# One layer of a hybrid decoder on one core: a fourth raw weight buffer, later second tables, a sum moved to VectorE and another order at the end

## The chip, the cores and the metric

The kernel runs on one core of one Trainium2 chip, in one launch. The metric is the device time of an execution in microseconds (us), told as the median of three runs. A profiled execution has its own time and a span: the span goes from the first recorded instruction to the last, and its own time is the span and the little that lies around it.

## What is computed

One decoder layer for 256 tokens of width 1024, in float32:

```python
h = x
h = h + hybrid_mixer(rmsnorm(h), ...)      # two attention branches, gates, output projection
h = h + peer_ffn(rmsnorm(h), wq, subkeys, u, v)
return rmsnorm(h, norm_final)

# peer_ffn: 128*128 = 16384 experts, 8 heads, 16 experts kept per head and token
q   = hf @ wq                              # scores against 2 x 128 subkeys per head
idx, w = top16 of the sums of two top16, softmax
act = gelu(einsum('cd,chkd->chk', x_c, u[idx]))
out = einsum('chk,chkd->cd', w * act, v[idx])
```

`u` and `v` have 16384 rows of 1024 numbers each, 64 MB apiece. The mixer takes some 270 us of the kernel; the change lies in the expert part.

## The kernel before, in words

**Weights.** All weight matrices are cut to blocks of 128 x 1024 float32 (512 KB) that stand in one list, `order`; the last 256 of them are 128 blocks of u and 128 of v. For each block SyncE (SP) issues one DMA into a tile `raw` (`fetch`, L184); ScalarE (ACT) rounds it to `whi` (L195) and VectorE (DVE) subtracts, `wlo = raw - whi` (L199), so that TensorE (PE) can multiply in two parts that together hold full precision. The pool `stream` has three buffers each for `raw`, `whi` and `wlo`. A `raw` buffer is free when `wlo` is made; a `whi` buffer when PE is through with that block. `slot` (L238) is the unit of the hand-written order: slot k issues the loads of blocks k+2 and k+3, makes `whi` and `wlo` of block k+2, runs what else is planned for this slot (lists `first`, `pre`, `late`, `early`), and then emits PE's matmuls for block k. The engines run their own rows in order and are tied by semaphores alone.

**u side.** Two blocks make a pair (`u_pair`): each block is multiplied with all tokens but the first 32 (24 matmuls of 224 columns, L367), the pair's result goes through Gelu to `G` (L1225, or L1219 and L1221). In the first half (64 blocks) the routing runs beside it: `steps` is a list of (estimated us, function) for top-16 searches, softmax, index lookups (`look_...`, ending in `idx`, L1047) and gathered dots; `advance(PACE)` at each slot gives it credit. `tables(b)` (L1049) transposes the weights and both index lists of token block b on PE (L1052) and copies them out. In the second half one-hot products (`hot_...`, L1294, L1309) multiply the routing weights into `G`.

**The first 32 tokens** are done otherwise: 32 times a row of u per partition (128 rows of 4 KB) is gathered by GpSimd (POOL) with an indirect DMA (L1086), `dot` (L1096) multiplies it on DVE with the tokens and gives a sum per row, and later 32 gathers of v are summed into `ysum` (`row_sum`, L1380). Dots 0 to 12 lie in the first half of u with three buffers, dots 13 to 21 in the second half and 22 to 31 in the first slots of the v side with two buffers `row0`, `row1` (`rows_wide`). Each dot or row_sum issues the gather that takes its buffer next (`rows_next`). After the last row_sum a chain on POOL folds the four parts (`fold_in`, `fold` L1392, `few_in` L1401 to L1403), `few_add` (L1406, POOL) adds the residual, `few_square` (L1409, ACT) and `few_factor` (L1414, ACT) give the norm, `few_out` (L1418 to L1424) writes the 32 rows. They are put at fixed slots of the v side by `at_slot`.

**v side.** Per block 8 matmuls of 448 columns with `whi` (`v_high`, L1345) and 8 of 224 with `wlo` (`v_low`, L1349) go into 8 PSUM banks `acc`; the moving operand `co` is made from `G` by ACT (L1258) and DVE (L1259) two slots ahead. The last two blocks are multiplied bank by bank (`finish`), DVE adds the residual (L1460, L1462), PE turns the rows (`turn_rows`, L1466), ACT sums squares (`total`, L1476), and norm and output follow (L1482 to L1518).

Of the kernel before, what the change touches and what calls it, by code (L numbers as in the profile page):

```python
# [31 lines left out]
PACE = 1.26  # L32
# [6 lines left out]
FETCH = 18  # L39
TD = T - NG  # L40
# [100 lines left out]
def body(tc, nc, a):  # L141
# [6 lines left out]
    ps = PP.enter_context(tc.tile_pool(name="ps", bufs=2, space=PSUM))  # L148
    PA = ExitStack()
# [22 lines left out]
    raws, parts, at = {}, {}, [0]  # L172

    def fetch(k):
        if k in raws or k >= len(order):
            return
        ap = order[k]
        t = stream.tile([P, D], F32, name="raw")
        if len(ap.shape) == 3:
            t = t[:, :ap.shape[1] * ap.shape[2]]  # L180
        raws[k] = t
        o = t if len(ap.shape) == 2 else t.rearrange("p (a b) -> p a b", a=ap.shape[1])
        if k:
# [54 lines left out]
    def slot(use, first=(), pre=()):  # L238
        k = at[0]
        fetch(k + 2)  # L240
        fetch(k + 3)
# [77 lines left out]
    ah = const.tile([P, NC, T], F32R)  # L319
    al = const.tile([P, NC, T], F32R)  # L320
# [760 lines left out]
    def rows_of_step(n):  # L1081
        return rows_at[n % 3] if n < DOTS[0] else rows_wide[n % 2]
# [6 lines left out]
    def rows_next(n):  # L1089
        m = n + (3 if n < DOTS[0] else 2)  # L1090
        if m < (DOTS[0] if n < DOTS[0] else 2 * NG):
            rows_in(m)
# [31 lines left out]
    steps.append((0.5, tables, 1))  # L1124
    first_dot = next(k for k, v in enumerate(steps) if v[1:] == (soft_sub, 1))
    ahead, behind = steps[:first_dot], steps[first_dot:]
    share, done, n = sum(v[0] for v in behind) / DOTS[0], 0.0, 0
    for v in behind:
        ahead.append(v)
        done += v[0]  # L1130
        while n < DOTS[0] and done >= share * (n + 0.5):
            ahead.append((1.35, dot, n))
            n += 1
    steps = ahead
# [47 lines left out]
    for m in range(8):  # L1182
        first, second = [], []
        if m:
# [8 lines left out]
            if m > 1:  # L1193
                first.append(lambda: advance(1.3))
                second.append(lambda: advance(0.6 if m == 2 else 1.2))
# [55 lines left out]
    rows_wide += [wide_rows.tile([P, D], F32, name=f"row{k}") for k in range(2)]  # L1251
# [8 lines left out]

    OH = ExitStack()
# [65 lines left out]
    for k in range(2):  # L1327
        at_slot(3 + 2 * k, "pre", rows_in, DOTS[0] + k)
# [8 lines left out]
    OH.close()  # L1337
    oh = top.enter_context(tc.tile_pool(name="ov", bufs=2, reuse_waits="tile"))
# [3 lines left out]
    small = slice(TD, 2 * TD)  # L1342

# [61 lines left out]
    def few_add():  # L1405
        nc.gpsimd.tensor_tensor(few[0], few[0], few[1], OP.add)  # L1406
# [18 lines left out]

    for n in range(DOTS[1], NG):
# [43 lines left out]
    sq = [oh.tile([P, 2], F32, name="lsq")[:TB] for b in range(2)]  # L1470
# [4 lines left out]
    def total(b, d):  # L1475
        nc.scalar.activation(whole, turned[2 * d + b][:TB], AF.Square, scale=1.0 / 32.0, accum_out=sq[b][:, d:d + 1])  # L1476
# [15 lines left out]
    def guard(b):  # L1492
        nc.vector.tensor_scalar(sums[b][:, 0:1], sq[b][:, 0:1], EPS, None, OP.add)

    rows_of = lambda b: a["out"][NG + b * TB:NG + (b + 1) * TB]
    for c in range(NC):
# [38 lines left out]
```

## Time and profile before

| | us |
|---|---|
| median of three runs (996.63, 1001.39, 1002.73) | 1001.39 |
| profiled execution, its own time | 995.05 |
| its span | 993.3 |
| u side, second half, first to last matmul | 464 to 651.6 |
| v side, first matmul L1345 to the first of `finish` | 651.59 to 974.87 |
| last output DMA issued | 987.72 |

All times within the execution count from the start of the span. A row of the chain or of a timeline is start, duration, engine, line, operation, output<-inputs; in brackets stands how long the engine was idle before it and what ended that. A row of a waits list is total us, times, longest. In a row of stretches the busy time and number of instructions of each engine come first, then the clock that TensorE was granted (1.00 is full), the mean busy share of the 16 DMA engines, and GB/s. PE's matmuls are pipelined: a busy PE shows only that work was in it.

### The profile page before, as it was taken

How to read it: one execution, taken by the hardware profiler on the slowest of the kernel's cores; microseconds unless marked ns; L12 is line 12 of the kernel's file. 1: busy time of each engine (PE TensorE's matmuls, PEld its weight loads, DVE VectorE, ACT ScalarE, POOL GpSimd, SP SyncE). 2: the span in 40 equal slices, each digit the busy share in tenths (PEclk: the TensorE clock that was granted, in tenths of full speed). 3: DMA queues.
4: the chain of work that ended last, by engine and by line, in shares of the span. 5: the costliest groups of instructions: out<-in, count | busy, mean ns of one | idle time of the engine just before them, and what ended most of it. 6: DMA issues, size and time to landing. Idle time of an engine off the chain costs nothing.

```text
span 993.3 us, 20220 instructions
## 1 busy us (share of the span) xinstructions
PE 971.9 (98%) x7825; PEld 940.1 (95%) x7825; DVE 793.9 (80%) x1485; ACT 591.1 (60%) x1069; POOL 130.8 (13%) x114
## 2 busy tenths in 40 slices
PE   9999999999999999999999999999999999999995
PEld 7898999999999999999999999999899999999985
DVE  5788877877989989877889999777777787777756
ACT  7545544656554655647888888655455555555553
POOL 3000110000000021221001001012212222223210
PEclk9999999999999999999999999999999999999998
DMA  8733344566556668877556555667888888888762
GB/s 276 255 94 119 109 116 144 170 197 176 182 182 213 217 205 276 300 261 239 197 182 208 191 192 191 212 230 258 274 280 288 279 307 284 285 296 300 267 213 82
DMA packets 61425, 217.24 MB, mean 219 GB/s; under 512 B 7121, under 2 KB 8321, under 8 KB 61321
## 3 DMA queue, kind: packets, MB, share of 16 engines
q1 hardware_dynamic: 48352, 174.42, 54.3%
q0 software_dynamic: 11280, 39.68, 11.4%
q10 hardware_dynamic: 1696, 1.84, 0.6%
q8 instruction: 62, 1.02, 0.4%
q14 instruction: 35, 0.28, 0.1%
HBM read 212.86 MB, written 2.52 MB: 217 GB/s over the span
## 4 chain that ended last, share of the span: by engine, by line
PE 56%; DMA 21%; DVE 13%; issue 5%; ACT 4%; POOL 1%; ACTq 0%; DVEq 0%; POOLq 0%
PE pj L367 45%; DMA raw<-in_v_n 16%; DVE wlo L199 6%; ACT whi L195 4%; PE pw L1294 3%; DMA raw<-in_u_t 2%; DVE ysum L1380 1%; DVE co L1259 1%; PE pS L660 1%; DMA xq<-ys 1%; PE pS L499 1%; PE pT L632 1%; PE acc L1345 1%; DMA row<-xrd 1%; DVE row L1096 1%
## 5 line engine op out<-in xcount | busy, mean ns | idle before, releaser
L199 DVE TENSOR_TENSOR wlo<-raw,whi 128x1024 fp32r<-128x1024 f32 (+2 forms) x329 | 398.3, 1211 | 131.7 <-ACT whi L195 130.1
L195 ACT ACTIVATE whi<-raw 128x1024 fp32r<-128x1024 f32 (+2 forms) x329 | 345.7, 1051 | 247.7 <-DMA raw<-in_v_n 92.9
L367 PE MATMUL pj<-ah,whi 128*128 128x224 f32 (+1 forms) x1344 | 320.6, 282 | 1.3 <-ACT ah L326 0.7
L367 PE MATMUL pj<-al,whi 128*128 128x224 f32 (+1 forms) x1344 | 314.9, 277 | 0.4 <-DVE al L327 0.4
L367 PEld LDWEIGHTS pj<-ah,whi 128*128 128x128 f32 x1344 | 257.4, 191 | 3.2 <-ACT ah L326 1.2
L367 PEld LDWEIGHTS pj<-al,whi 128*128 128x128 f32 x1344 | 258.0, 192 | 2.0 <-issue 1.0
L1345 PE MATMUL acc<-co,whi 128*128 128x448 f32 x1024 | 232.7, 368 | 4.4 <-ACT whi L195 4.3
L1345 PEld LDWEIGHTS acc<-co,whi 128*128 128x128 f32 x1024 | 183.3, 189 | 17.5 <-ACT whi L195 5.7
L367 PE MATMUL pj<-ah,wlo 128*128 128x224 f32 (+1 forms) x1344 | 181.5, 277 | 0.0
L367 PEld LDWEIGHTS pj<-ah,wlo 128*128 128x128 f32 x1344 | 166.7, 192 | 0.0
L1349 PEld LDWEIGHTS acc<-co,wlo 128*128 128x128 f32 x1024 | 134.9, 191 | 4.2 <-DVE wlo L199 0.9
L1349 PE MATMUL acc<-co,wlo 128*128 128x224 f32 x1024 | 136.2, 273 | 0.6 <-DVE wlo L199 0.6
L1282 ACT ACTIVATE onehot<-onehot,wl 128x128 f16<-128x128 f16 x224 | 71.3, 393 | 6.1 <-DVE onehot L1286 3.9
L1086 POOL DMA_INDIRECT row<-in_v_n,sidx x32 | 51.6, 1612 | 157.8 <-DVE ysum L1380 116.8
L1258 ACT ACTIVATE co<-G 128x224 fp32r<-128x224 f32 x128 | 48.8, 382 | 32.1 <-PE acc L1349 31.4
L1086 POOL DMA_INDIRECT row<-in_u_n,sidx x19 | 29.7, 1565 | 225.1 <-DVE row L1096 224.5
L1259 DVE TENSOR_TENSOR co<-G,co 128x224 fp32r<-128x224 f32 x128 | 49.7, 389 | 8.9 <-ACT co L1258 8.9
L367 PE MATMUL pj<-bh,whi 128*128 128x256 f32 x192 | 48.0, 286 | 0.0
L367 PE MATMUL pj<-bl,whi 128*128 128x256 f32 x192 | 47.4, 284 | 0.0
L1380 DVE SCALAR_TENSOR_TENSOR ysum<-row,acts,ysum 128x1024 f32<-128x1024 f32 x31 | 39.6, 1279 | 0.0
L627 ACT ACTIVATE prob<-pS,nm 128x128 f32<-128x128 f32 (+1 forms) x48 | 19.8, 416 | 30.6 <-DVE nm L624 30.6
L367 PEld LDWEIGHTS pj<-bl,whi 128*128 128x128 f32 x192 | 36.5, 190 | 0.0
(323 smaller groups left out, 931.1 us busy)
## 6 DMA issues: line engine op xcount, KB each, us to landing
raw<-in_u_t SPq DMA_DIRECT2D x128, 512.0 KB, 3.6
raw<-in_v_n SPq DMA_DIRECT2D x128, 512.0 KB, 4.7
raw<-in_w_m SPq DMA_DIRECT2D x16, 512.0 KB, 3.6
raw<-in_w_q SPq DMA_DIRECT2D x16, 512.0 KB, 3.7
raw<-in_w_t SPq DMA_DIRECT2D x15, 512.0 KB, 4.6
raw<-in_w_b SPq DMA_DIRECT2D x8, 512.0 KB, 3.5
raw<-in_w_o SPq DMA_DIRECT2D x8, 512.0 KB, 3.5
sg<-in_w SPq DMA_DIRECT2D x4, 512.0 KB, 6.5
```

Source lines behind the costliest of these rows:

```text
L195: return [lambda s=slice(u, min(v, n)): nc.scalar.activation(hi[:, s], raws[k][:, s], AF.Copy) for u, v in cuts]
L199: nc.vector.tensor_tensor(lo[:, cs], raws[k][:, cs], hi[:, cs].bitcast(F32), OP.subtract)
L367: nc.tensor.matmul(out, (wl if v == 2 else wh)[:, c], (l if v == 1 else h)[:, c], start=(i == 0), stop=(i == len(seq) - 1))
L627: nc.scalar.activation(p[:, o], src[b], AF.Exp, bias=nm[:, b:b + 1], accum_out=sums[:, b, h:h + 1])
L1086: nc.gpsimd.indirect_dma_start(rows_of_step(n), None, src, bass.IndirectOffsetOnAxis(ap=sidx[:, n % NG:n % NG + 1], axis=0))
L1258: nc.scalar.activation(t[:, :TD], g, AF.Copy)
L1259: nc.vector.tensor_tensor(t[:, TD:], g, t[:, :TD].bitcast(F32), OP.subtract)
L1282: nc.scalar.activation(E[:, 1, t], E[:, 1, t], AF.Copy, scale=wl[:, n:n + 1])
L1294: nc.tensor.matmul(pw[:, t * P:(t + 1) * P], E[:, 0, t], E[:, 2 - s, t], start=(s == 0), stop=(s == 1))
L1345: nc.tensor.matmul(acc[c][:, :2 * TD], w[0][:, c * P:(c + 1) * P], coefs[k], start=(k == 0), stop=False, skip_group_check=True)
L1349: nc.tensor.matmul(acc[c][:, small], w[1][:, c * P:(c + 1) * P], coefs[k][:, :TD], start=False, stop=(k == P - 1), skip_group_check=True)
L1380: nc.vector.scalar_tensor_tensor(ysum, t, w, ysum, OP.mult, OP.add)
```

## The change

**Four raw buffers.** From block 67 of u on, of every four weight blocks three go to the pool `stream` as before and the fourth to a spare buffer in the pool `rows`; from the second half of u on, `slot` issues the loads of blocks k+2 to k+4. **One row buffer in the second half of u.** Only `row0` is there; the second, `row1`, is made at the start of the v side in the pool that takes the place of the one-hot tiles, and its first gather (row 23) is issued in slot 0 there. `ah` and `al` (the tokens in two parts) move to a pool of their own that closes after the u side. **Second tables last.** `tables(1)` stands at the end of `steps`, behind all dots; `PACE` is 1.29 for 1.26, and the last of the eight query pairs gives less credit. **The gathered tokens' sum** (`few_add`) is made by DVE, in slot 118 instead of 112; the table load for the square root, `few_square`, `few_factor` and `few_out` come five slots later each, `few_in` one. **The end.** In `finish` both `whi` products come ahead of both `wlo` products, the residual is added to the large part first, and the squares of the second half of the columns are summed in two pieces (384 and 128 columns).

```diff
-PACE = 1.26
+PACE = 1.29
+SPARE = 1
...
+    spares, V0, ahead = [], len(order) - P - 61, [3]
     def fetch(k):
...
-        t = stream.tile([P, D], F32, name="raw")
+        spare = spares and (k - V0) % (3 + SPARE) >= 3
+        t = (spares[0] if spare else stream).tile([P, D], F32, name="raw", **({"bufs": SPARE} if spare else {}))
...
     def slot(use, first=(), pre=()):
         k = at[0]
-        fetch(k + 2)
-        fetch(k + 3)
+        for n in range(2, ahead[0] + 1):
+            fetch(k + n)
...
     def rows_of_step(n):
-        return rows_at[n % 3] if n < DOTS[0] else rows_wide[n % 2]
+        return rows_at[n % 3] if n < DOTS[0] else rows_wide[n % len(rows_wide)]
...
     def rows_next(n):
-        m = n + (3 if n < DOTS[0] else 2)
+        m = n + (3 if n < DOTS[0] else len(rows_wide))
...
-    steps.append((0.5, tables, 1))
...
-    steps = ahead
+    steps = front + [(0.5, tables, 1)]
...
-                first.append(lambda: advance(1.3))
-                second.append(lambda: advance(0.6 if m == 2 else 1.2))
+                first.append(lambda: advance(1.3 if m < 7 else 1.0))
+                second.append(lambda: advance(0.6 if m in (2, 7) else 1.2))
...
-    rows_wide += [wide_rows.tile([P, D], F32, name=f"row{k}") for k in range(2)]
+    rows_wide.append(wide_rows.tile([P, D], F32, name="row0"))
...
+    spares.append(wide_rows)
+    ahead[0] = 3 + SPARE
...
-    for k in range(2):
-        at_slot(3 + 2 * k, "pre", rows_in, DOTS[0] + k)
+    at_slot(3, "pre", rows_in, DOTS[0])
...
     OH.close()
+    HX.close()
...
+    rows_wide.append(oh.tile([P, D], F32, name="row1", bufs=1))
...
     def few_add():
-        nc.gpsimd.tensor_tensor(few[0], few[0], few[1], OP.add)
+        nc.vector.tensor_tensor(few[0], few[0], few[1], OP.add)
...
+    at_slot(0, "v", rows_in, DOTS[1] + 1)
...
-    at_slot(n + 4, "v", few_in)
-    at_slot(n + 6, "v", few_add)
-    at_slot(n + 9, "v", lambda: table(AF.Sqrt))
-    at_slot(n + 10, "v", few_square)
-    at_slot(n + 11, "v", few_factor)
-    at_slot(n + 13, "v", few_out)
+    at_slot(n + 5, "v", few_in)
+    at_slot(n + 12, "v", few_add)
+    at_slot(n + 14, "v", lambda: table(AF.Sqrt))
+    at_slot(n + 15, "v", few_square)
+    at_slot(n + 16, "v", few_factor)
+    at_slot(n + 18, "v", few_out)
...
     def finish(c):
-        for k in (P - 2, P - 1):
-            v_high(k, ends[k], c)
-            v_low(k, ends[k], c)
+        for f in (v_high, v_low):
+            for k in (P - 2, P - 1):
+                f(k, ends[k], c)
         xc = x2c(c)[:, NG:]
-        nc.vector.tensor_tensor(xc, xc, acc[c][:, small], OP.add)
         lasts[c] = oh.tile([P, TD], F32, name="last", bufs=3)
-        nc.vector.tensor_tensor(lasts[c], acc[c][:, :TD], xc, OP.add)
+        nc.vector.tensor_tensor(xc, xc, acc[c][:, :TD], OP.add)
+        nc.vector.tensor_tensor(lasts[c], acc[c][:, small], xc, OP.add)
...
     turn_rows(6)
+    for b in range(2):
+        total(b, 4, 7, 1)
     turn_rows(7)
     for b in range(2):
+        gained(b, 0)
         guard(b)
-        gained(b, 0)
     for b in range(2):
-        total(b, 1)
+        total(b, 7, 8, 2)
         root(b)
```

How the change moves rows is shown at three places. The first is DVE at the end of the first half of u, where the last index list `idx` is made; `wlo` rows are the weight blocks, `xg` and `g_wide` rows are dots, `wl` belongs to `tables(1)`. Before:

```order
L199 TENSOR_TENSOR wlo<-raw,whi 128x1024 [waits DMAHW6_49,PE_49,Activation_49]
L1096 SCALAR_TENSOR_TENSOR g_wide,acts<-g_wide,xq 128x1024 [waits DMASW0_49]
L199 TENSOR_TENSOR wlo<-raw,whi 128x1024 [waits DMAHW7_49,PE_49,Activation_49]
L1046 TENSOR_TENSOR sc<-sc 128x8x32 [waits DVE_49]
L1047 TENSOR_TENSOR idx<-sc 128x128 [waits DVE_49]
L1061 SCALAR_TENSOR_TENSOR wl<-pO,wt 128x128 [waits PE_49,Activation_49]
L199 TENSOR_TENSOR wlo<-raw,whi 128x1024 [waits DMAHW0_49,Activation_49]
L1096 SCALAR_TENSOR_TENSOR xg,acts<-xg,xq 128x1024 [waits DMASW1_49]
```

And now:

```order
L204 TENSOR_TENSOR wlo<-raw,whi 128x1024 [waits DMAHW6_49,PE_49,Activation_49]
L1101 SCALAR_TENSOR_TENSOR g_wide,acts<-g_wide,xq 128x1024 [waits DMASW0_49]
L1051 TENSOR_TENSOR sc<-sc 128x8x32 [waits DVE_49]
L1052 TENSOR_TENSOR idx<-sc 128x128 [waits DVE_49]
L204 TENSOR_TENSOR wlo<-raw,whi 128x1024 [waits DMAHW7_49,PE_49,Activation_49]
L1101 SCALAR_TENSOR_TENSOR xg,acts<-xg,xq 128x1024 [waits DMASW1_49]
L204 TENSOR_TENSOR wlo<-raw,whi 128x1024 [waits DMAHW0_49,PE_49,Activation_49]
L1066 SCALAR_TENSOR_TENSOR wl<-pO,wt 128x128 [waits PE_49,Activation_49]
```

`idx` is one weight block earlier on DVE, and the last dot and the table's own row have changed places. On PE the three transposes of `tables(1)` stand one weight block (24 matmuls) later than before.

The second place is ACT near the end of the v side, slots 115 to 117 before: the table load, the square of the 32 rows and the root. Before:

```order
L195 ACTIVATE whi<-raw 128x1024 [waits DMAHW5_49,DVE_49]
L280 ACT_TABLE_LOAD
L280 ACTIVATE junk<-ones 128x1
L1258 ACTIVATE co<-G_5867 128x224 [waits DVE_49,PE_49]
L195 ACTIVATE whi<-raw 128x1024 [waits DMAHW6_49,DVE_49]
L1409 ACTIVATE row_5872,fs<-row_5871 32x1024 [waits DMASW4_49,DMASW5_49,DMASW2_49,Pool_49]
L1258 ACTIVATE co<-G_5867 128x224 [waits DVE_49,PE_49]
```

Now, at slots 120 to 122:

```order
L200 ACTIVATE whi<-raw 128x1024 [waits DMAHW2_49,DVE_49]
L285 ACT_TABLE_LOAD
L285 ACTIVATE junk<-ones 128x1
L1262 ACTIVATE co<-G_5870 128x224 [waits DVE_49,PE_49]
L200 ACTIVATE whi<-raw 128x1024 [waits DMAHW3_49,DVE_49]
L1416 ACTIVATE row_8860,fs<-row_5874 32x1024 [waits DMASW4_49,DMASW5_49,DMASW2_49,DVE_49]
L1262 ACTIVATE co<-G_5870 128x224 [waits DVE_49,PE_49]
```

The square waits for DVE, no longer for POOL, and stands five blocks later; the row that it waits for stands on DVE three blocks ahead of it.

The third place is PE at the start of `finish`, the last two blocks of v, first two banks (the numbers behind the names are buffers: `whi_12070` and `wlo_12071` are the last block but one, `whi_12093` and `wlo_12094` the last). Before:

```order
L1345 MATMUL acc_8855<-co_12067,whi_12070 128x448
L1349 MATMUL acc_8855<-co_12067,wlo_12071 128x224
L1345 MATMUL acc_8855<-co_12090,whi_12093 128x448
L1349 MATMUL acc_8855<-co_12090,wlo_12094 128x224
L1345 MATMUL acc_8854<-co_12067,whi_12070 128x448
L1349 MATMUL acc_8854<-co_12067,wlo_12071 128x224
```

Now (`whi_12067` and `wlo_12068` the last block but one, `whi_12097` and `wlo_12098` the last):

```order
L1352 MATMUL acc_8859<-co_12064,whi_12067 128x448
L1352 MATMUL acc_8859<-co_12094,whi_12097 128x448
L1356 MATMUL acc_8859<-co_12064,wlo_12068 128x224
L1356 MATMUL acc_8859<-co_12094,wlo_12098 128x224
L1352 MATMUL acc_8858<-co_12064,whi_12067 128x448
L1352 MATMUL acc_8858<-co_12094,whi_12097 128x448
```

The product with the last `whi` moves from the third place of a bank to the second; the one with the last `wlo` stays the fourth. SP's list of loads and POOL's list of gathers keep their order, but that rows 23 and later are asked for at other steps; POOL loses the sum.

More of the change, by code (lines that the diff above doesn't have):

```diff
@@ L148, in body @@
     ps = PP.enter_context(tc.tile_pool(name="ps", bufs=2, space=PSUM))
+    HX = ExitStack()
+    hx = HX.enter_context(tc.tile_pool(name="hx", bufs=1, side="right", reuse_waits="tile"))
     PA = ExitStack()
@@ L318, in body @@
     x2c = lambda c: x2[c // 4][:, c % 4]
-    ah = const.tile([P, NC, T], F32R)
-    al = const.tile([P, NC, T], F32R)
+    ah = hx.tile([P, NC, T], F32R, name="ah")
+    al = hx.tile([P, NC, T], F32R, name="al")
     bh = pa.tile([P, NC, T], F32R)
@@ L1123, in body @@
             steps.append((0.3, route))
-    steps.append((0.5, tables, 1))
     first_dot = next(k for k, v in enumerate(steps) if v[1:] == (soft_sub, 1))
-    ahead, behind = steps[:first_dot], steps[first_dot:]
+    front, behind = steps[:first_dot], steps[first_dot:]
     share, done, n = sum(v[0] for v in behind) / DOTS[0], 0.0, 0
     for v in behind:
-        ahead.append(v)
+        front.append(v)
         done += v[0]
         while n < DOTS[0] and done >= share * (n + 0.5):
-            ahead.append((1.35, dot, n))
+            front.append((1.35, dot, n))
             n += 1
-    steps = ahead
+    steps = front + [(0.5, tables, 1)]
     credit = [0.0]
@@ L1424, in few_out @@
         nc.gpsimd.dma_start(a["out"][0:NG], few[0])
+    assert DOTS[1] % 2 == 0
+    at_slot(0, "v", rows_in, DOTS[1] + 1)
     for n in range(DOTS[1], NG):
@@ L1469, in body @@
     yo = [stream.tile([P, D], F32, name="raw")[:TB] for b in range(2)]
-    sq = [oh.tile([P, 2], F32, name="lsq")[:TB] for b in range(2)]
+    sq = [oh.tile([P, 4], F32, name="lsq")[:TB] for b in range(2)]
     sums = [oh.tile([P, 4], F32, name="lr")[:TB] for b in range(2)]
@@ L1473, in body, with total @@
     whole = rows_wide[1][:TB, 0:512]
-    def total(b, d):
-        nc.scalar.activation(whole, turned[2 * d + b][:TB], AF.Square, scale=1.0 / 32.0, accum_out=sq[b][:, d:d + 1])
+    def total(b, c0, c1, n):
+        d = c0 // 4
+        cs = slice((c0 - 4 * d) * P, (c1 - 4 * d) * P)
+        nc.scalar.activation(whole[:, cs], turned[2 * d + b][:TB, cs], AF.Square, scale=1.0 / 32.0,
+                             accum_out=sq[b][:, n:n + 1])
     def gained(b, d):
@@ L1481, in root @@
     def root(b):
-        nc.scalar.activation(sums[b][:, 1:2], sq[b][:, 1:2], AF.Sqrt, bias=sums[b][:, 0:1])
+        nc.scalar.activation(sums[b][:, 1:2], sq[b][:, 2:3], AF.Sqrt, bias=sums[b][:, 0:1])
     def factor(b):
         e, r, w, t = (sums[b][:, k:k + 1] for k in range(4))
-        nc.vector.tensor_scalar(w, sq[b][:, 1:2], e, -0.5, OP.add, OP.mult)
+        nc.vector.tensor_scalar(w, sq[b][:, 2:3], e, -0.5, OP.add, OP.mult)
         nc.vector.reciprocal(r, r)
@@ L1492, in guard @@
     def guard(b):
-        nc.vector.tensor_scalar(sums[b][:, 0:1], sq[b][:, 0:1], EPS, None, OP.add)
+        nc.vector.scalar_tensor_tensor(sums[b][:, 0:1], sq[b][:, 0:1], EPS, sq[b][:, 1:2], OP.add, OP.add)
     rows_of = lambda b: a["out"][NG + b * TB:NG + (b + 1) * TB]
@@ L1501, in body @@
             for b in range(2):
-                total(b, 0)
+                total(b, 0, 4, 0)
     turn_rows(6)
+    for b in range(2):
+        total(b, 4, 7, 1)
     turn_rows(7)
     for b in range(2):
+        gained(b, 0)
         guard(b)
-        gained(b, 0)
     for b in range(2):
-        total(b, 1)
+        total(b, 7, 8, 2)
         root(b)
```

## The prediction

> **What bounds the kernel now.** I read the page's first lines, then the waits of PE, then stretches around each wait.
>
> ```profile
> span 993.3 us, 20220 instructions
> PE 971.9 (98%) x7825; PEld 940.1 (95%) x7825; DVE 793.9 (80%) x1485; ACT 591.1 (60%) x1069; POOL 130.8 (13%) x114
> ```
>
> PE has work in it for 971.9 of 993.3 us. The change takes no matmul away, so at most what PE waits, and what it runs at a low clock, can be won: 21 us, much of it in the mixer's start, which the change leaves alone. The waits of PE from 285 us on (total, times, longest):
>
> ```profile
> PE acc L1345 <- ACT whi L195: 4.3, 5, 2.2
> PE pO L1052 <- DVE idx L1047: 2.2, 1, 2.2
> PE pj L367 <- ACT whi L195: 0.6, 1, 0.6
> PE acc L1349 <- DVE wlo L199: 0.6, 1, 0.6
> PE acc L1466 <- DVE lr L1493: 0.4, 1, 0.4
> ```
>
> Each row belongs to one part of the change: the second tables (L1052), the expert weights (L1345), the end (L1349, L1466). The list counts only waits that a semaphore shows, so the v side is also measured by its pace. Its first blocks on the chain of waits, and the first product of `finish`:
>
> ```profile
> 651.75 1.63 PE acc L1345 x8
> ...
> 656.77 1.63 PE acc L1345 x8
> ...
> 974.87 0.38 PE L1345 MATMUL acc<-co,whi 128*128 128x448 f32 x1
> ```
>
> A block that waits for nothing takes (656.77 - 651.75) / 2 = 2.51 us. From 651.59 (the start that the table of the kernel before gives) to 974.87 are 323.3 us for 126 blocks; 126 x 2.51 = 316.3. With the rounding of the period some **6.7 us** are lost on the v side. The stretches say where:
>
> ```profile
> 444.00:447.00 3.00, 0.96 (x9) 0.96 (x10) 1.72 (x3) 0.80 (x4) 0.00 (x0) 1.00 0.52 161
> 447.00:448.00 1.00, 1.00 (x10) 1.00 (x9) 0.29 (x1) 1.00 (x3) 0.00 (x0) 0.79 0.92 373
> 448.00:451.00 3.00, 3.00 (x16) 3.00 (x16) 2.68 (x4) 1.67 (x3) 0.01 (x1) 0.50 0.20 55
> ...
> 687.00:730.00 43.00, 41.43 (x258) 38.91 (x259) 30.99 (x45) 22.60 (x36) 7.82 (x5) 1.00 0.77 258
> 730.00:750.00 20.00, 20.00 (x129) 19.05 (x128) 15.03 (x20) 11.20 (x17) 3.85 (x3) 1.00 0.88 304
> 950.00:960.00 10.00, 7.80 (x48) 7.10 (x47) 2.59 (x5) 4.37 (x9) 2.40 (x1) 1.00 0.53 186
> ```
>
> From 687 to 730 PE starts late again and again (43.00 - 41.43 = 1.6 us idle; a late block also costs a little behind it), and the DMA engines have a share of only 0.77 there, while from 730 to 750 PE waits for nothing at 0.88 and 304 GB/s. So loads come late there because they are asked for late, not because the engines are full. The granted clock is 0.50 from 448 to 451, right behind the wait for `idx`.
>
> **The second tables.** PE stands at L1052 until DVE has made `idx`:
>
> ```profile
> 443.14 1.06 ACT L195 ACTIVATE whi<-raw 128x1024 fp32r<-128x1024 f32 x1 [2.87 <-DMA raw<-in_u_t]
> 443.60 0.27 PE L1052 MATMUL pO<-ident,idx 128*128 128x128 f32 x1
> 445.69 0.29 DVE L1047 TENSOR_TENSOR idx<-sc 128x128 f32<-128x128 bf16 x1
> 446.04 0.33 PE L1052 MATMUL pO<-ident,idx 128*128 128x128 f32 x1 [2.17 <-DVE idx L1047]
> 457.30 0.69 DVE L1286 TENSOR_TENSOR onehot<-onehot,wt 128x1024 f16<-128x1024 f16 x1
> ```
>
> Now `idx` stands ahead of one `wlo` (1.2 us) on DVE, and PE comes one block (24 products, about 2.7 us) later: together 3.9 us against a wait of 2.17, so it goes. What is late next is that block's `whi`, ready at 443.14 + 1.06 = 444.2 when PE would want it at 443.6 or soon after: I leave 0.5 us. The wait also cost clock: 1.0 x 0.21 + 3.0 x 0.50 = 1.7 us of full-speed work. Term: 2.2 + 1.7 - 0.5 = **3.4 us**; bounds 1.7 (the clock drops all the same) and 3.9 (no wait is left). The last dot and the moved table rows are the same rows in another order; the first row that reads the tables, DVE's one-hot tile at 457.30, stands 11 us behind 446.04, so a block's delay there costs nothing.
>
> [...]
>
> **Earlier load in the first half.** At 295 us PE waits 0.6 us (L367 above) on
>
> ```profile
> 294.56 1.06 ACT L195 ACTIVATE whi<-raw 128x1024 fp32r<-128x1024 f32 x1 [6.38 <-DMA raw<-in_u_t]
> ```
>
> The last query pair's smaller credit moves DVE's searches behind the `wlo` that frees this load's buffer. I take **0.4** (bounds 0 and 0.6). `PACE` 1.29 puts the same rows into fewer slots: nothing, since DVE is busy for 80% of the span (and if a slot were full, its `wlo` would come late and PE wait).
>
> **Four raw buffers.** The rows of `raw` on the v side, and ACT's wait for it:
>
> ```profile
> L195 ACT ACTIVATE whi<-raw x126: 1039/1062/1067, 652.8 to 973.8; 128x1024 fp32r<-128x1024 f32 x126
> L199 DVE TENSOR_TENSOR wlo<-raw,whi x126: 1206/1225/1227, 653.9 to 974.8; 128x1024 fp32r<-128x1024 f32 x126
> DMA to landing us min/median/max: 3.2/4.8/7.9
> ...
> ACT whi L195 <- DMA raw<-in_v_n: 92.9, 67, 3.7
> ```
>
> A buffer's round is landing, `whi` 1.06, `wlo` 1.23 and about 0.2 of handing over (estimated from the spacing of these rows). With three buffers a round has 3 x 2.51 = 7.53 us, so 5.0 are left for landing: the median of 4.8 just fits, 7.9 does not, and ACT waits for 67 of 126 loads. With four there are 10.04 - 2.5 = 7.5 us. Nearly every load then fits, and the credit saved over three good blocks pays for a bad one. SP issues the same 128 loads in the same order, each one a buffer earlier; nothing else waits behind them on SP in this stretch. Of the 6.7 us the next part takes 2.9; the other 3.8 are late loads, and shrink to about 0.6: **3.2** (bounds 0 and 3.8).
>
> **The sum on VectorE.** The largest single wait of the v side is near 956:
>
> ```profile
> ACT row L1409 <- POOL row L1406: 5.7, 1, 5.7
> 926.57 0.58 POOL L1383 DMA_DIRECT2D ys<-ysum  x1 [10.80 <-DVE co L1259]
> 951.86 2.40 POOL L1406 TENSOR_TENSOR row<-row,row 32x1024 f32<-32x1024 f32 x1 [4.55 <-DMA row<-xrd]
> 954.29 1.05 ACT L1409 ACTIVATE row<-row 32x1024 f32<-32x1024 f32 x1 [5.67 <-POOL row L1406]
> 956.72 1.48 PE L1345 MATMUL acc<-co,whi 128*128 128x448 f32 x6 [2.20 <-ACT whi L195]
> ```
>
> ACT stands 5.67 us at the square because POOL's sum comes late; `whi` rows queue behind it, and PE, its lead used up, waits 2.2 us (10.00 - 7.80 in the stretch above). I put the loss at 2.9, with an estimated 0.7 for the two blocks behind, whose `whi` come late as well. The chain from 926.57 to its last input at 951.86 takes 25.3 us. Now the sum is planned 12 slots, 30.1 us, behind the last `ysum` (924.99 in the old order, counted to the start of DVE's row), so the input is there some 3 to 5 us early, and the square comes three blocks behind the sum. The sum on DVE costs between 1.2 (its 128x1024 rows above) and 2.4 us (POOL's row); DVE has room:
>
> ```profile
> 900.00:950.00 50.00, 50.00 (x321) 47.69 (x320) 36.88 (x45) 28.56 (x41) 12.82 (x11) 1.00 0.84 275
> ```
>
> 13.1 us idle of 50. Without that cover a late input would stop DVE in order, `wlo` rows behind it, and PE after two blocks. I take all **2.9** (bounds 0 and 2.9). `few_out` moves to four blocks ahead of the end on DVE, which is behind the next term. Both parts on the v side: **6.1** (bounds 2.9, if the loads give nothing, and 6.7).
>
> **One row buffer in the second half of u, two on v.** Gathers there:
>
> ```profile
> row<-in_u_n,sidx POOLq DMA_INDIRECT x19, 6.0
> row<-in_v_n,sidx POOLq DMA_INDIRECT x32, 6.6
> 661.84 1.22 DVE L1096 SCALAR_TENSOR_TENSOR row<-row,xq 128x1024 f32<-128x1024 f32 x1
> ```
>
> In the second half a dot comes every 6 slots. By the table of the kernel before, 64 slots take 651.6 - 464 = 187.6 us, so 17.6 us lie between dots, against 6.0 of landing, 1.2 of dot and some 1.6 of issue: cost 0, where without the cover each dot would wait. `row1` is asked for in slot 0 of v, and its dot 23 stands at 661.84 in the trace of before, ten us behind the first block: 0.
>
> **The end.** The profile has
>
> ```profile
> 976.13 0.37 PE L1349 MATMUL acc<-co,wlo 128*128 128x224 f32 x1 [0.56 <-DVE wlo L199]
> 983.78 0.60 ACT L1476 ACTIVATE row<-acc 112x512 f32<-112x512 f32 x1 [1.47 <-PE acc L1466]
> ```
>
> The product that needs the last `wlo` stays fourth in its bank, and `few_out` is now nearer, so 0.56 stays. The residual adds still wait for the whole bank. The squares that end last read 128 columns for 512: each of the 0.60 us rows shrinks (by an estimated 0.3 to 0.4), but the pieces of 384 now run ahead of the last transposes, which wait for them on the same bank. I take **0.3** (bounds 0 and 0.8).
>
> **Sum.** 3.4 + 0.4 + 6.1 + 0.3 = 10.2 us: span 993.3 - 10.2 = 983.1, with the 1.75 around it (995.05 less 993.3) **984.85** against 995.05 for the profiled execution. The median of the runs lies 6.3 above that execution, and no trace shows why. If late loads make it, the fourth buffer takes it too; if not, it stays. I take half: 984.85 + 3.2 = **988.0 us**.
>
> **Rivals.** *The engines are full:* the v side needs 512 KB per 2.51 us and a gather of 512 KB per 6.28 us, together 292 GB/s, next to the 304 of the best stretch. Then a fourth load in flight only lands later, and the 3.2 are not won: sum 7.0, execution 988.05, with the half gap 991.3. For it: landing already reaches 7.9. Against it: 304 GB/s went without a wait. [...]
>
> *The clock drops all the same*, because few rows run on PE around the tables wherever they stand, or the wait goes to `whi`: the first term is 1.7, the sum 8.5, 986.55, with the half gap 989.7. For it: a wait of the same length near 956 left the clock at 1.00, so the wait alone does not decide. Against it: it is the only low spell after 285 us, and it starts behind the longest wait.
>
> *Slower: the gathers starve.* In the first slots of v the rows land late already:
>
> ```profile
> DMA to landing us min/median/max: 5.0/7.9/9.2
> 671.24 0.94 POOL L1086 DMA_INDIRECT row<-in_u_n,sidx  x1 [5.93 <-DVE row L1096]
> 682.94 1.22 DVE L1096 SCALAR_TENSOR_TENSOR row<-row,xq 128x1024 f32<-128x1024 f32 x1
> ```
>
> From a gather's issue to its dot 11.7 us pass; up to that landing a longer one costs nothing, beyond it DVE stops in order, all else behind. If a fourth load stretches all transfers as the longest load stretches the median (7.9 / 4.8 = 1.65), 7.9 becomes 13.0 (the gain is used up from about 12.2 on): 1.3 us per round of two row steps, 41 steps on the v side, 27 us; execution 1011.9, with the half gap 1015. Against it: four loads ask for no more bytes per us, so the stretch should be short of that.
>
> *The fourth buffer isn't used as meant*, since its loads wait for something else: sum 7.0, 991.3 as for full engines.
>
> **Chances.** Forecast 0.58, engines full 0.18, clock 0.15, gathers 0.06, buffer not used 0.03. One per cent below the median is 991.4; about that much a measurement of this kernel can tell from no change. The forecast lies between 984.9 and 991.2 with none or all of the gap; I count 0.48 of its 0.58 as faster by over 1%, 0.08 of the clock's 0.15, 0.06 of 0.18 and 0.01 of 0.03: 0.63. Slower by over 1%: 0.05 of the gathers' 0.06. Within 1%: 0.32. **Range:** the low end has all terms at their upper bounds (3.9 + 0.6 + 6.7 + 0.8 = 12.0: 983.05) and none of the gap, less the 1.6 by which the lowest run and the profiled execution differ: 981. The high end has full engines and the clock together (5.3: 989.75), all of the gap (996.05) and a little of the 1.6: 997. It leaves out the gathers.
>
> **What the changed profile would show.** Tables: no wait at the table transposes, no granted clock under 1.00 near 445 to 455. Loads: ACT's wait for `raw<-in_v_n` far below 92.9 us, issue to landing longer than 4.8, and blocks of 2.51 from 651 to 970. Sum: no wait of ACT at the square, no wait of DVE at the sum. Gathers: no wait of DVE at dots or `ysum`. Wrong would be: PE idle over 2 us on the v side, a row of DVE that waits for `row`, or a clock spell elsewhere.

## The result and the profile after

The changed kernel takes 983.87 us in the median (983.33 to 985.88), the kernel before 1001.59 (996.63 to 1002.73); the ratio is 0.9836, interval 0.98 to 0.9872. The profiled execution of the changed kernel takes 983.33 us with a span of 981.6, so its median lies 0.5 us above the profiled one, where the kernel before has 6.5 (6.3 by the three runs that were known first). On a later chip two of the kernel before's 13 executions (1004.46 and 1007.55 us) count as slow and are left out of its figures there.

The first lines of the page after:

```profile
span 981.6 us, 20226 instructions
PE 968.7 (99%) x7825; PEld 938.1 (96%) x7825; DVE 801.7 (82%) x1486; ACT 587.0 (60%) x1073; POOL 141.4 (14%) x113
```

The span is 11.7 us shorter, PE's idle time 12.9 us for 21.4. The waits of PE from 285 us on are three rows now, all of them at the end:

```profile
PE acc L1475 <- ACT row L1487: 0.9, 2, 0.6
PE acc L1356 <- DVE wlo L204: 0.5, 1, 0.5
PE acc L1475 <- DVE last L1471: 0.3, 1, 0.3
```

The wait for `idx`, the wait at 295 us and all five for `whi` of the v side are gone. The same stretches as before (the first two are the second tables, the next two were the late loads and the good blocks behind them, the last was the wait for the sum) show PE busy throughout and the clock at 1.00:

```profile
444.00:447.00 3.00, 3.00 (x29) 3.00 (x28) 3.00 (x5) 1.55 (x4) 0.58 (x1) 1.00 0.62 232
447.00:451.00 4.00, 4.00 (x38) 4.00 (x38) 2.75 (x4) 1.82 (x3) 0.98 (x1) 1.00 0.89 271
687.00:730.00 43.00, 43.00 (x275) 41.00 (x274) 33.17 (x46) 23.20 (x37) 10.36 (x6) 1.00 0.80 281
730.00:750.00 20.00, 20.00 (x130) 19.07 (x129) 15.88 (x20) 10.63 (x17) 5.83 (x4) 1.00 0.84 287
950.00:960.00 10.00, 10.00 (x66) 9.53 (x65) 6.41 (x10) 7.25 (x13) 0.00 (x0) 1.00 0.51 150
```

On the v side the first rows below say what ACT waits for over the whole execution (total, times, longest); the other two are from the view of the tile `raw` between 651 and 975 us:

```profile
ACT co L1262 <- PE acc L1356: 141.7, 122, 1.5
ACT whi L200 <- PE pj L372: 50.9, 52, 4.8
ACT whi L200 <- DMA raw<-in_u_t: 35.4, 21, 4.7
...
  DMA raw<-in_v_n: 0.2, 1
DMA to landing us min/median/max: 2.4/4.7/7.8
```

The loads land as late as before (4.7 in the median and 7.8 at the longest, against 4.8 and 7.9; the prediction had looked for more than 4.8), but 92.9 us of ACT's waiting for them became 0.2. ACT now waits for PE, which is how it should look where PE sets the pace.

For the comparison of all runs I divided each profiled execution at five rows of PE in its trace: the first product of u, the first product of u's block 61, the first one-hot product, the first product of v, and the first of `finish`. Each number is the difference of two starts, in us:

| kernel | to u | u, 60 blocks | tables | u, rest | v | `finish` to the end | profiled execution |
|---|---|---|---|---|---|---|---|
| before | 275.20 | 162.93 | 25.79 | 187.67 | 323.28 | 18.41 | 995.05 |
| after | 274.79 | 162.09 | 21.77 | 187.67 | 316.68 | 18.56 | 983.33 |
| three_raw | 277.06 | 162.09 | 21.78 | 187.67 | 326.36 | 18.56 | 995.30 |
| only_raw | 276.29 | 162.14 | 22.31 | 187.67 | 316.68 | 17.84 | 984.71 |
| no_gather | 275.37 | 162.09 | 21.78 | 187.67 | 316.68 | 18.29 | 983.64 |
| tables_old | 274.88 | 165.04 | 23.50 | 187.67 | 316.68 | 18.51 | 988.06 |
| first_old | 275.19 | 162.32 | 26.04 | 187.67 | 316.68 | 18.49 | 988.16 |
| all_again | 275.80 | 163.29 | 21.78 | 187.55 | 316.67 | 18.50 | 985.36 |
| wait_long | 275.22 | 162.40 | 21.77 | 187.67 | 323.12 | 17.44 | 989.48 |
| sum_old | 275.79 | 163.71 | 21.87 | 187.67 | 317.44 | 17.44 | 985.79 |
| out_early | 274.64 | 162.09 | 21.78 | 187.67 | 316.68 | 17.41 | 982.04 |
| early_again | 275.47 | 162.09 | 21.78 | 187.67 | 316.68 | 17.43 | 982.89 |
| all_third | 274.82 | 162.09 | 23.09 | 187.55 | 316.68 | 18.47 | 984.47 |

Between the first two rows the 11.7 us are 0.4 ahead of u (kernels with the same code up to there lie between 274.64 and 277.06, so this says nothing), 0.8 in u's first blocks, 4.0 at the tables, 0 in the rest of u, 6.6 on the v side, and 0.15 lost at the end.

### The profile page after: what moved, and what is told of

Its sections match the earlier page's. It is cut to its first block, busy times and chain, and to the rows that moved or that the text cites. A ratio compares the mean times of both kernels' runs of the same rounds, so it can differ in the third digit from the quotient of the medians.

```text
span 981.6 us, 20226 instructions
## 1 busy us (share of the span) xinstructions
PE 968.7 (99%) x7825; PEld 938.1 (96%) x7825; DVE 801.7 (82%) x1486; ACT 587.0 (60%) x1073; POOL 141.4 (14%) x113
## 4 chain that ended last, share of the span: by engine, by line
PE 94%; DVE 4%; issue 1%; ACT 1%; DMA 0%; DVEq 0%; ACTq 0%
PE pj L372 52%; PE acc L1352 21%; PE acc L1356 11%; PE pw L1300 3%; DVE wlo L204 1%; PE pS L665 1%; PE pS L504 1%; PE pT L637 1%; PE pS L1166 1%; DMA raw<-in_w_t 0%; PE pO L648 0%; PE pO L649 0%; PE pj L769 0%; PE pj L767 0%; PE pj L766 0%
## 5 line engine op out<-in xcount | busy, mean ns | idle before, releaser
L1091 POOL DMA_INDIRECT row<-in_v_n,sidx x32 | 62.3, 1945 | 146.4 <-DVE ysum L1387 115.3
L1263 DVE TENSOR_TENSOR co<-G,co 128x224 fp32r<-128x224 f32 x128 | 50.2, 393 | 21.4 <-ACT co L1262 21.1
L1091 POOL DMA_INDIRECT row<-in_u_n,sidx x19 | 32.9, 1730 | 218.2 <-DVE row L1101 217.6
L632 ACT ACTIVATE prob<-pS,nm 128x128 f32<-128x128 f32 (+1 forms) x48 | 19.7, 416 | 30.6 <-DVE nm L629 30.6
```

What stands on the lines that cost most here:

```text
L632: nc.scalar.activation(p[:, o], src[b], AF.Exp, bias=nm[:, b:b + 1], accum_out=sums[:, b, h:h + 1])
L1091: nc.gpsimd.indirect_dma_start(rows_of_step(n), None, src, bass.IndirectOffsetOnAxis(ap=sidx[:, n % NG:n % NG + 1], axis=0))
L1263: nc.vector.tensor_tensor(t[:, TD:], g, t[:, :TD].bitcast(F32), OP.subtract)
```

## The experiments

The kernels three_raw, only_raw, out_early and tables_old shared one chip, where the kernel before had a median of 996.16; all_again, first_old, no_gather and wait_long a second (999.49); sum_old, early_again and all_third a third (997.71). Diffs are against the changed kernel unless the text says otherwise.

**Three raw buffers, all else as changed.**

```diff
-    spares.append(wide_rows)
-    ahead[0] = 3 + SPARE
```

> The changed kernel with three raw buffers again (no spare; the single row buffer in the second half of u and all else stay). Theory A (the ring of three buffers is too short for the landing, and also makes the runs lie above the profiled execution): on the v side ACT waits some 90 us for raw again, PE loses about 3.8 us against the 316.6 us that the v side takes now, so the profiled execution is about 987 us, and the median of the runs lies 3 to 6 us above it, near 991. Rival B (late loads followed from the wait for POOL's sum and from the order of the gathers, not from the number of buffers): v side within 1 us of 316.6, execution 983 to 985, runs the same.

Median 991.82 us (989.63 to 995.66), ratio to before 0.9956 (0.9923 to 0.9989); profiled 995.30, v side 326.36. PE's and ACT's rows, and the tile `raw` on the v side:

```profile
PE acc L1350 <- ACT whi L200: 6.3, 10, 1.4
...
ACT whi L200 <- DMA raw<-in_v_n: 121.1, 70, 4.3
...
DMA to landing us min/median/max: 3.2/4.9/7.8
```

The v side loses 9.7 us. PE's ten waits for the `whi` of late loads are 6.3 of it, the rest shows as no wait of PE's, and none is at the sum. Theory A holds for the cause, B falls. A missed twice: the loss was more than its 3.8, and the median lies 3.5 us below the profiled execution and not 3 to 6 above it. That late loads are not the same from run to run (the runs lie 6 us apart) fits both misses. All other parts of the change together are worth 0.4% here.

**The fourth raw buffer alone.** Against the kernel before this has only the spare buffer, the three loads ahead, the pool of `ah` and `al`, and the row buffers:

```diff
...
+    spares, V0, ahead = [], len(order) - P - 61, [3]
...
-    rows_wide += [wide_rows.tile([P, D], F32, name=f"row{k}") for k in range(2)]
+    rows_wide.append(wide_rows.tile([P, D], F32, name="row0"))
...
+    spares.append(wide_rows)
+    ahead[0] = 3 + SPARE
```

> The kernel before with the fourth raw buffer and the single row buffer in the second half of u alone; tables, pace, sum on POOL and end as before. Theory A: the v side loses only the 2.9 us of the wait for the sum, ACT's wait for raw all but goes, the profiled execution is about 995 - 3.8 = 991.3 us and the runs lie within 2 us of it (992 to 993), so that a large part of the gain of the runs comes from this part alone. Rival B: the profiled execution stays near 995 and the runs near 1000.

Median 984.54 us (984.25 to 987.69), ratio 0.9862 (0.981 to 0.9915): nearly the whole gain, and more than A expected. The v side has the full 316.68 though POOL makes the sum in its old slot:

```profile
ACT row L1417 <- POOL row L1414: 2.2, 1, 2.2
```

ACT still stands there, for 2.2 us where it was 5.7, and PE does not notice. The tables in their old order cost little as well:

```profile
PE pO L1057 <- DVE idx L1052: 0.3, 1, 0.3
```

So two waits that the prediction booked to other parts of the change came short or cost nothing in this execution, which has the old order at both places. That asked for the next three experiments.

**The tables in their old place**, then **the whole first half as before**. The first has

```diff
+    steps.append((0.5, tables, 1))
     front, behind = steps[:first_dot], steps[first_dot:]
...
-    steps = front + [(0.5, tables, 1)]
+    steps = front
```

and the second beside it

```diff
-PACE = 1.29
+PACE = 1.26
...
-                first.append(lambda: advance(1.3 if m < 7 else 1.0))
-                second.append(lambda: advance(0.6 if m in (2, 7) else 1.2))
+                first.append(lambda: advance(1.3))
+                second.append(lambda: advance(0.6 if m == 2 else 1.2))
```

> The changed kernel with tables(1) in its old place ahead of the last dots, PACE and credits as changed. Theory: PE waits about 2.2 us for idx again and the granted clock falls to 0.50 for some 3.4 us behind it; the first half ends 3.5 to 4.0 us later, execution about 987. [...]

One run, 988.06. PE waits for `idx` 1.4 us, and the clock stays at 1.00 (stretches of tables_old; the wait ends at 447.18):

```profile
PE pO L1057 <- DVE idx L1052: 1.4, 1, 1.4
...
445.00:447.00 2.00, 0.76 (x7) 0.52 (x6) 1.97 (x5) 0.57 (x1) 0.00 (x0) 1.00 0.60 174
447.00:449.00 2.00, 1.82 (x16) 1.83 (x17) 1.55 (x3) 1.46 (x4) 0.00 (x0) 1.00 0.56 221
```

1.7 us are lost at the tables, less than the theory's 3.5; the other 3 us lie in u's blocks ahead of them, where PE waits 2.1 us for ACT.

> The changed kernel with the whole first half of u as before: tables(1) ahead of the last dots, PACE 1.26, old credits. Theory C (the wait for idx was 2.2 us in the profile of before because a weight load came late ahead of it; with loads on time it is 0.3 us, as in the run with four raw buffers alone): median 0.5 to 1 us above the changed kernel, single runs up to 4 us above. Rival (the prediction's term: the order itself costs 3.4 to 4.0, and the load at 295 us 0.4 to 0.85): median 987.5 to 988.5.

Median 987.03 us (984.77 to 990.96), the changed kernel on the same chip 985.35 (983.37 to 987.39). Two of its six runs lie near 991, one near 988, three near 985: it looks less like a price than like a chance. The profiled one is of the dear kind (26.04 us at the tables). What stood ahead of `idx` there, on ACT and DVE:

```profile
442.78 1.06 ACT L200 ACTIVATE whi<-raw 128x1024 fp32r<-128x1024 f32 x1 [2.36 <-DMA raw<-in_u_t]
443.87 1.23 DVE L204 TENSOR_TENSOR wlo<-raw,whi 128x1024 fp32r<-128x1024 f32 x1 [1.48 <-ACT whi L200]
445.34 0.29 DVE L1052 TENSOR_TENSOR idx<-sc 128x128 f32<-128x128 bf16 x1
...
447.00:448.00 1.00, 1.00 (x6) 1.00 (x6) 0.29 (x1) 1.00 (x3) 0.00 (x0) 0.50 0.76 303
```

A load came late, ACT stood 2.36 us for it, DVE 1.48 at that block's `wlo`, and `idx` queued behind. The profile of before has the same three rows at 443.14, 444.23 and 445.69, the first with 2.87 us for the load. So theory C holds for the cause as far as four profiles with the old order show it: ACT stood 0 us (only_raw), 1.45 (tables_old), 2.36 and 2.87 for the load of the last block ahead of `idx`, and PE then waited 0.3, 1.4, 2.4 and 2.2. But it takes the order too. In none of the nine profiles with the new order does PE wait for `idx`, though ACT stood 4.06 us (changed kernel) and 5.00 (all_third) for the load of the block ahead of it. In all_third PE waits 1.1 us there for a Gelu row instead, and the tables take 23.09 us. In size the medians are 1.7 us apart, which lies between C and the rival; with six runs each whose ranges overlap, and with `PACE` and the credits undone as well, this is no measured price of the order.

**The v side without its gathers, three raw buffers.** Only the first two gathers of the v side are issued, so the output for the first 32 tokens is left out; the dots and sums run all the same.

```diff
-    spares.append(wide_rows)
-    ahead[0] = 3 + SPARE
...
-        if m < (DOTS[0] if n < DOTS[0] else 2 * NG):
+        if m < (DOTS[0] if n < DOTS[0] else DOTS[1] + 2):
```

> The changed kernel with three raw buffers, and on the v side only the first two of the 41 gathers: the later dots and sums read rows that already lie there (the output for the first 32 tokens is left out). Theory A in its stronger form (the landing of a load is lengthened by the gathers on the same DMA engines, so that three buffers do not suffice): landing falls from 4.8 to about 3.6 us as on the u side, ACT's wait for raw falls far below 90 us, and the v side takes within 1 us of 316.7. Rival (the pace of 512 KB per 2.51 us alone is too much for three buffers): landing stays over 4.3 us and the v side loses several us again.

One run, 983.64; the v side takes 316.68 with three buffers. The tile `raw` from 655 to 960 us:

```profile
  DMA raw<-in_v_n: 2.4, 4
DMA to landing us min/median/max: 4.0/4.3/4.8
```

Landing fell to 4.3 and not to 3.6 (the median of the u blocks in before), so the gathers are not all of the difference; what makes the rest was not tried. But what changed most is the longest, 4.8 for 7.8, and that is just under the 5.0 us that three buffers leave. Theory A in the stronger form holds: the gathers make single loads late, and it is those that three buffers cannot carry. Whether it is their transfers or POOL's rows for them is not separated. A page's median would not have told it.

**A long wait at the square.** The sum on POOL in its old slot 112, the square in 113:

```diff
-        nc.vector.tensor_tensor(few[0], few[0], few[1], OP.add)
+        nc.gpsimd.tensor_tensor(few[0], few[0], few[1], OP.add)
...
-    at_slot(n + 5, "v", few_in)
-    at_slot(n + 12, "v", few_add)
-    at_slot(n + 14, "v", lambda: table(AF.Sqrt))
-    at_slot(n + 15, "v", few_square)
-    at_slot(n + 16, "v", few_factor)
-    at_slot(n + 18, "v", few_out)
+    at_slot(n + 4, "v", few_in)
+    at_slot(n + 6, "v", few_add)
+    at_slot(n + 6, "v", lambda: table(AF.Sqrt))
+    at_slot(n + 7, "v", few_square)
+    at_slot(n + 11, "v", few_factor)
+    at_slot(n + 13, "v", few_out)
```

> The changed kernel with the sum on POOL in its old slot and the square eight slots earlier (slot 113), so that ACT must wait about 9 us for the sum. Theory (with four raw buffers PE has two blocks, about 5 us, in hand, which is why ACT's wait of 2.2 us cost nothing in the run with four raw buffers alone): PE waits 3.5 to 5 us, the v side takes that much more than 316.7, and behind so long a gap the granted clock falls to 0.50 for some 3.4 us (1.7 us more). Rival (four buffers hide such a wait whole): v side within 1 us of 316.7. [...]

One run, 989.48, v side 6.4 us longer:

```profile
PE acc L1352 <- ACT whi L200: 3.8, 1, 3.8
...
ACT row L1416 <- POOL row L1413: 7.3, 1, 7.3
...
942.00:944.00 2.00, 1.39 (x4) 1.26 (x5) 1.45 (x3) 2.00 (x5) 0.00 (x0) 0.50 0.00 0
944.00:946.00 2.00, 2.00 (x8) 1.78 (x7) 2.00 (x4) 1.01 (x2) 0.00 (x0) 0.50 0.56 168
```

ACT stands 7.3 us and PE 3.8: PE has 3.5 us in hand when ACT stops. That is the same figure as in the profile of before, 5.7 less 2.2. So the fourth buffer adds nothing to this lead (`whi` has three buffers in both kernels); the wait of before mattered since the chain to the sum was late. The clock stood at 0.50 for 6.8 us and not the expected 3.4, which makes up the rest of the 6.4. From `ys` to POOL's sum it took 25.3 us in the profile of before, 20.0 here, 22.9 in sum_old below, and in the run with four raw buffers alone 22.4:

```profile
919.12 0.58 POOL L1391 DMA_DIRECT2D ys<-ysum  x1 [10.62 <-DVE co L1264]
941.56 2.37 POOL L1414 TENSOR_TENSOR row<-row,row 32x1024 f32<-32x1024 f32 x1 [4.15 <-DMA row<-xrd]
```

**The sum and its chain in the old place**, all else as changed:

```diff
-        nc.vector.tensor_tensor(few[0], few[0], few[1], OP.add)
+        nc.gpsimd.tensor_tensor(few[0], few[0], few[1], OP.add)
...
-    at_slot(n + 5, "v", few_in)
-    at_slot(n + 12, "v", few_add)
-    at_slot(n + 14, "v", lambda: table(AF.Sqrt))
-    at_slot(n + 15, "v", few_square)
-    at_slot(n + 16, "v", few_factor)
-    at_slot(n + 18, "v", few_out)
+    at_slot(n + 4, "v", few_in)
+    at_slot(n + 6, "v", few_add)
+    at_slot(n + 9, "v", lambda: table(AF.Sqrt))
+    at_slot(n + 10, "v", few_square)
+    at_slot(n + 11, "v", few_factor)
+    at_slot(n + 13, "v", few_out)
```

> The changed kernel with the gathered tokens' sum back on POOL and the old slots of table load, square, factor and few_out (sum in slot 112, square 116). Theory D (PE has 3.5 us in hand when ACT stands at the square, and with four buffers the chain to the sum is 2 to 3 us shorter than in the profile of before, so the move of the sum is worth nothing on the v side; but few_out far from the end frees DVE for the last wlo): ACT waits 2 to 4 us at the square, PE under 0.5, v side 316.7 to 317.2, tail about 1 us shorter than the changed kernel's, so the execution is 0 to 1 us below the changed kernel. Rival (the prediction's term): 2.9 us above it.

Median 983.18 us (982.32 to 985.79) against 984.28 for the changed kernel on this chip (983.36 to 985.66). The v side loses 0.8 us (317.44; D had 0 to 0.5), ACT waiting 3.5 at the square, and the end gains 1.0 (17.44 for 18.47). Theory D holds but for that 0.8: moved as it was, the sum's chain is worth nothing, since its last part lands on the end. The times alone could not tell 1 us; the stretches of the traces do.

**The chain of the sum earlier, on DVE.**

```diff
-    at_slot(n + 12, "v", few_add)
-    at_slot(n + 14, "v", lambda: table(AF.Sqrt))
-    at_slot(n + 15, "v", few_square)
-    at_slot(n + 16, "v", few_factor)
-    at_slot(n + 18, "v", few_out)
+    at_slot(n + 10, "v", few_add)
+    at_slot(n + 11, "v", lambda: table(AF.Sqrt))
+    at_slot(n + 12, "v", few_square)
+    at_slot(n + 13, "v", few_factor)
+    at_slot(n + 14, "v", few_out)
```

> The changed kernel with the chain of the gathered tokens earlier: sum two slots earlier (116), table load, square, factor three, three and three slots earlier, and few_out in slot 120 for 124. Theory: few_out's 1.3 us on DVE is what delays the last co and the last wlo now (PE's waits of 0.5 and about 0.3 at the start of finish); free of it the execution is 0.7 to 1.0 us shorter, about 982.5, and no wait comes at the sum since its input lands 6 us early. Rival: the last wlo is late of itself, as it was before with few_out five slots away: execution 983.3 as now.

> The changed kernel with the chain of the gathered tokens earlier, once more beside the changed kernel on one chip. Theory: its tail is 17.4 us against 18.5, no other stretch differs, so the median is 1.1 us below the changed kernel's, with runs 1 to 3 us apart by late loads in the first half. Rival: the difference of the earlier run was chance, 0.

> The changed kernel itself, as the base for the others of this chip. Expected 983.3 to 984.5 us in the median, its runs within 3 us of each other, v side 316.7 us without a wait; the kernel before 993 to 1002 with a wide spread.

> The changed kernel, the base of these two on their chip: median 983.5 to 985.5 us, v side 316.7, tail 18.5.

Medians 983.11 (982.04 to 983.29) and, beside the changed kernel's 984.28, 983.36 (982.77 to 985.73). The end takes 17.41 and 17.43 us, in the changed kernel 18.56, 18.50 and 18.47; no other stretch differs by design, and the v side is 316.68 in both. Why the changed kernel's end is longer, on DVE and PE:

```profile
961.71 1.27 DVE L1430 SCALAR_TENSOR_TENSOR row<-row,fs,xq 32x1024 f32<-32x1024 f32 x1
962.91 0.37 DVE L1263 TENSOR_TENSOR co<-G,co 128x224 fp32r<-128x224 f32 x1
963.21 1.21 DVE L204 TENSOR_TENSOR wlo<-raw,whi 128x1024 fp32r<-128x1024 f32 x1
...
964.48 0.37 PE L1356 MATMUL acc<-co,wlo 128*128 128x224 f32 x1 [0.50 <-DVE wlo L204]
```

`few_out` (L1430) stands ahead of the last `co` and the last `wlo`. With it four slots earlier, the last `wlo` starts 0.9 us ahead of the first product of `finish` (962.85), where in the changed kernel it starts 0.2 behind it (963.00):

```profile
961.92 1.23 DVE L204 TENSOR_TENSOR wlo<-raw,whi 128x1024 fp32r<-128x1024 f32 x1 [0.56 <-ACT whi L200]
```

and PE waits for none. The ratios to before are 0.984 (0.979 to 0.989) and 0.9855 (0.9816 to 0.9893). It beats the changed kernel by about 1 us in the traces, which the times bear out (0.9 in the median) without settling it; sum_old, with 983.18 on the same chip, is as fast. The changed kernel as base ran as expected on the third chip; on the second its 985.35 lay 0.9 above the expected bound, and its runs 4 us apart where 3 was expected.

## Why the prediction was right, point by point

The forecast of 988.0 us lay 4.1 above the measured 983.87, the range held it, and it was faster by over 1%. The sum against the profiled execution was 10.2 us, measured 11.7; 0.4 of that lies ahead of u and is within what kernels of the same code differ by there. That the sum came so near is in part luck: as the points below show, its split was wrong.

- **Second tables, 3.4 predicted, 4.0 in the pair of profiles.** No wait was left for the `whi` behind, where 0.5 was put. But the wait was taken for a property of the order alone, and it also takes a late load ahead of `idx`: 0.3 us when the load is on time, 1.4, 2.2 and 2.4 when it is not. In the profiles the old order takes 22.31 to 26.04 us at the tables, the new one 21.77 to 21.87 in eight of nine and 23.09 in the ninth; the medians of runs (1.7 apart, first_old against all_again) do not settle its worth.
- **Load in the first half, 0.4 predicted, 0.8 in the pair.** The step held: in the three profiles with the old credits (before, only_raw, first_old) this block's `whi` starts 18.6 to 19.4 us after the first product of u, in the ten with the new ones 16.9 to 18.1. In the changed kernel ACT waits there for PE and no longer for the load:

```profile
292.07 1.06 ACT L200 ACTIVATE whi<-raw 128x1024 fp32r<-128x1024 f32 x1 [4.80 <-PE pj L372]
```

  But PE's wait of 0.6 us came in only one of those three (only_raw and first_old have 162.14 and 162.32 us for the 60 blocks), so the term is a chance too. Kernels with the new credits lose elsewhere in these blocks: all_again (163.29) and sum_old (163.71) show PE's waits 140 to 153 us after the first product of u. The first half still has three raw buffers; that late loads make this rest was not tried.
- **Four raw buffers, 3.2 of the 6.1 predicted; 6.6 measured.** The ring arithmetic was right: landing unchanged, 5.0 us of room too little and 7.5 enough, though the longest load took 7.8. The split was wrong. The fourth buffer alone takes all 6.6 (only_raw), and more in runs with more late loads (9.7 in three_raw).
- **The sum on VectorE, 2.9 predicted.** Here the step failed: with loads on time the chain to the sum is about 3 us shorter, ACT's wait stays near the 3.5 us that PE has in hand, and moving the sum brings 0 to 0.8 on the v side. The prediction took two waits in one execution for two separate causes. Whether late loads made the chain of before longer stays open. From `ys` to the issue of the sum's last input it took 19.7 us in before and 19.0 in three_raw, 14.5 to 18.2 with four buffers, but also 18.6 in no_gather, whose loads were on time.
- **The end, 0.3 predicted, -0.15 measured.** The new order at the end does bring about 0.4 (17.44 in sum_old against only_raw's 17.84, which differ in the end's order alone among what bears on it); its parts were not separated. `few_out` in slot 124 takes 1.1. The prediction saw that it comes nearer and left the 0.56 us wait as it was; it did not count that `co` queues behind it too.
- **The gap between median and profile, half of 6.3 predicted to go; 6.0 of 6.5 went.** This is the largest miss, and part of it is luck of the four runs of before: on the three later chips its medians are 996.16, 999.49 and 997.71, that is 1.1 to 4.4 above its profiled 995.05. Where both kernels ran again the gain is 14.1 and 13.4 us (ratios 0.9866 and 0.9859), and the forecast, 13.4 below 1001.39, had just that, by a sum whose split was wrong. The prediction left open whether late loads make the spread. The runs support it: with three buffers all through, runs of before lie 987 to 1002 us on one chip, three_raw 990 to 996, and kernels with the fourth buffer and the new order 982 to 987.4. Only the profiled executions show the loads themselves.
- **Rivals.** *Engines full* fell: landing stayed at 4.7 us at 281 to 287 GB/s, and nothing waited. *The clock drops all the same* fell in the changed kernel (1.00 from 444 to 451 us). *The fourth buffer isn't used* fell: ACT's wait for loads of v went from 92.9 us to 0.2. *Gathers starve* fell: landing of the gathers of v went from a median of 6.6 to 7.2, under the 11.7 us that they have, and no row of DVE waits for one.

```profile
row<-in_v_n,sidx POOLq DMA_INDIRECT x32, 7.2
row<-in_u_n,sidx POOLq DMA_INDIRECT x19, 6.6
```

## What to carry to other kernels

Size a ring of load buffers by the longest landing, not the median: buffers x period less the work on a buffer should come near it. Here 5.0 us of room lost nothing with a longest landing of 4.8 and 6.6 to 9.7 us with one of 7.8 or 7.9, and 7.5 lost nothing with 7.8. With the gathers beside the loads the longest landing was 7.8 for 4.8 and the median only 4.9 for 4.3 (three_raw, no_gather). Before giving each wait of one profile to a part of the change, ask whether one late transfer stands behind several of them, and whether a second execution has them at all: runs that lie far apart, as those of before do, are a hint that such chance waits exist, and the profiled execution can be at either end of them. Work moved off one path to a place near the end of the kernel has to be counted against the rows that are last there.

## What the runs showed of the hardware

The length of PE's gap alone did not decide the clock in these runs. A gap of 1.4 us left it at 1.00 (tables_old); gaps of 2.2 and 2.4 at the tables were followed by 0.50 (before, first_old), and one of 3.8 had 0.50 before it ended (wait_long: from 940.80 on, PE's next product at 942.61); a gap of 2.2 near 956 us in the profile of before left it at 1.00. In the clock records of before the spell of 0.50 at the tables lasts 3.413 us, from 447.59 to 451.00, and the next one starts at 986.89, that is 539.30 us or 158 such lengths behind the start of the first. Divided at whole lengths of 3.413 us from 447.59, before has around its two gaps

```profile
444.17:447.59 3.42, 1.55 (x14) 1.55 (x15) 1.93 (x4) 1.22 (x5) 0.00 (x0) 1.00 0.57 194
447.59:451.00 3.41, 3.41 (x19) 3.41 (x18) 2.76 (x5) 2.08 (x3) 0.01 (x1) 0.50 0.28 90
...
952.76:956.17 3.41, 1.76 (x13) 1.52 (x11) 0.39 (x1) 1.88 (x4) 1.50 (x1) 1.00 0.44 178
956.17:959.59 3.42, 2.87 (x17) 2.57 (x17) 1.79 (x4) 2.08 (x5) 0.00 (x0) 1.00 0.17 43
```

and wait_long, divided from the start of its spell, where two lengths in a row have little work on PE,

```profile
937.38:940.80 3.42, 1.39 (x11) 1.17 (x9) 0.00 (x0) 0.62 (x1) 2.35 (x1) 1.00 0.50 200
940.80:944.21 3.41, 1.60 (x4) 1.47 (x5) 2.02 (x4) 3.41 (x8) 0.00 (x0) 0.50 0.00 0
944.21:947.62 3.41, 3.41 (x14) 3.19 (x14) 2.48 (x3) 0.80 (x1) 0.00 (x0) 0.50 0.71 192
```

A length with PE busy for 1.55 us at full clock was followed by 0.50 in before, one with 1.39 in wait_long; the one with 1.76 in before was not. In first_old PE was busy for 1.57 of the 4 us from 443 to 447, with a mean clock of 0.84, and the clock was 0.50 from 447 to 449; in tables_old it was busy for 2.58 of the 4 us from 445 to 449, all at 1.00. The gap near 956 us is split between two of these lengths, the one at the tables lies almost whole in one. That this is why only one of the two cost clock is an estimate from these few rows; no run here moved a gap on purpose.

POOL's rows for the v gathers had a mean of 1945 ns with four raw buffers for 1612 before, without a cost, and the loads did not land later with one more of them asked for (4.7 us in the median for 4.8): only the time at which they are asked for moved.
